# Layer norms of a decoder step: centring on TensorE, next weights split before the last tile, affine on ScalarE, mean shift inside the chain

## The chip, the cores and the metric

The kernel runs on one core of a Trainium2 chip as a single launch. A core has TensorE (PE, matrix products), VectorE (DVE), ScalarE (ACT), GpSimd (POOL) and SyncE (SP, which here issues most DMAs). The metric is device time in microseconds for one execution; the median of three runs is given for the kernel before.

## The reference

One inference step of a two-layer decoder, for 256 prompt tokens and 8 sample tokens together (264 columns). Model width 1024, FFN width 2816, four heads, 256 memory tokens.

```python
DN_ALPHA = (2 * DEPTH) ** 0.25                       # DEPTH = 2
def layer_norm(x, g, b):
    mu = jnp.mean(xf, -1, keepdims=True)
    var = jnp.mean(jnp.square(xf - mu), -1, keepdims=True)
    return (xf - mu) * lax.rsqrt(var + LN_EPS) * g + b
def trunk(x, ...):
    for l in range(DEPTH):
        x = layer_norm(DN_ALPHA * x + 0.5 * swiglu(x, gate[l, 0], up[l, 0], down[l, 0]), ln_g[l, 0], ln_b[l, 0])
        if l % 2 == 0: mix = gdn_conformer_mixer(x, ...)      # gated DeltaNet beside a convolution module
        else:          mix, gm_v = chunk_mlp_mixer(x, ...)    # gMLP with spatial gating
        x = layer_norm(DN_ALPHA * x + mix, ln_g[l, 1], ln_b[l, 1])
        x = layer_norm(DN_ALPHA * x + cross_attend(x, ...), ln_g[l, 2], ln_b[l, 2])
        x = layer_norm(DN_ALPHA * x + 0.5 * swiglu(x, gate[l, 1], up[l, 1], down[l, 1]), ln_g[l, 3], ln_b[l, 3])
```

Outputs are the new x of both groups, the keys and values of the memory, and the new states of the mixer. So there are eight layer norms over x. The text numbers them 0 to 7: norms 0, 3, 4 and 7 stand behind an FFN, norms 1, 2, 5 and 6 behind an output projection (mixer, attention 0, gMLP, attention 1).

## The kernel before

x lies transposed: eight tiles k = 0..7 of 128 channels by 264 tokens. Every large product is done in float32 accuracy by three products of rounded parts. A weight column block `raw` (1024 x 256, loaded by SP, three buffers) is cut into units of 128 output channels; ScalarE rounds one to `whi` (L221), VectorE or GpSimd subtracts and gives `wlo` (L222), with four buffers of each. The right-hand side is `xhi`, `xlo` likewise. A unit is 24 products on TensorE (8 tiles k, three each, L605) into one of four PSUM buffers `mm`, so a unit can start only when the unit four before it has been read out of PSUM.

A norm (class `Norm`) goes like this.

- `add` (L282) puts alpha times x plus the PSUM of output tile k into x. At k = 1 a rough mean is taken from the first two tiles (one product with `ones`, L289); ScalarE copies it twice, as `lnca` and `lnc` (L292, L293), GpSimd subtracts `lnca` from the six tiles still to come (L295), VectorE `lnc` from the first two (L297). `acc` then makes `xpre` (x times the gain, hi on ScalarE L313 and lo on VectorE L314) and adds to the running sums `lnS` (L320) and `lnQ` (squares, L319 and L321; the last two tiles on VectorE, the earlier ones on GpSimd).
- `finish` lets the next layer's products start on `xpre` before the norm is known: the true result is linear in it, so that a unit's PSUM is mended afterwards (`fixed`: L345 adds the mean's part, L346 multiplies by 1/sigma). Units 0 to 3 and some fillers (key and value products of a cross-attention, "K units", `Filler`) run there. After 18 products of unit 0 come the `sums`: three transposes of `lnS` (L149), the product that gives the remaining mean shift `dl` (L330), three transposes of `lnQ`. VectorE, with one square root on ScalarE (L110), turns them into 1/sigma as a diagonal `dg` (L135), and one product L137 spreads it over all partitions; it is called the spread below.
- Behind the spread x is made whole: x plus `lndl` (L367; VectorE for k < 2, GpSimd for the other six), times 1/sigma (L383), `xhi` with gain and bias (ScalarE L384), x itself with gain and bias (ScalarE L386; for k = 0, 2, 5 VectorE L392), `xlo` (L394; GpSimd for k = 3, 5, 7). Between them stand the fixes of units 0 to 7 at the steps `at`, and units 4 to 7 open as the fixes free their PSUM.
- `split_w` takes entries of the list `after_norm`: the `wlo` of two of units 0 to 3 goes to GpSimd (of 2 and 3, in front of an FFN of 1 and 3); the first two weights split after a norm wait until the square root and `dg` have been issued.

Each engine works its instructions off in order. That order is the program's, except where a scheduler at build time moves instructions; `pin` keeps those named in program order. The last norm has its own end (`finish_out`) and no `xpre`.

## Time and profile before

| | |
|---|---|
| median of 3 runs | 1422.63 us (1422.1 to 1422.78) |
| profiled execution, its own time | 1418.37 us |
| its span in the trace | 1416.6 us |
| granted TensorE clock, mean over the span | 0.975 of full |
| busy: PE, DVE, ACT, POOL | 1345.7, 952.9, 735.6, 317.1 us |

The profile is one execution; all durations below are from it, and it took 4.26 us less than the median. PE stands for TensorE's products, a window gives for each engine its busy time and in brackets the number of instructions that were recorded, then the granted TensorE clock, where 1.00 is the level of 2.4 GHz and 0.50 that of 1.2 GHz. "[1.89 <-DVE dg L135]" behind an instruction says that its engine had been idle for 1.89 us and what ended this.

### The profile page before, as it was taken

The numbers are of one execution on the slowest core, as the hardware profiler recorded it, in microseconds if no ns is written. First come the engines' busy times: TensorE is split into PE (matmuls) and PEld (weight loads), VectorE is DVE, ScalarE is ACT, GpSimd is POOL, SyncE is SP. The second block draws the span as 40 slices with busy tenths as digits, with TensorE's granted clock in tenths as the row PEclk, the third lists the DMA queues.
The fourth block names the chain that finished last, engine by engine and source line by source line (L and its number), as shares of the span: only waits on it lengthen the run. The fifth ranks groups of instructions, "written<-read, shape, count | busy, mean of one in ns | idle before, by whom it ended". The sixth has DMA issues, their size and how long they took to land.

```text
span 1416.6 us, 27334 instructions
## 1 busy us (share of the span) xinstructions
PE 1345.7 (95%) x10931; PEld 1276.2 (90%) x10931; DVE 952.9 (67%) x1845; ACT 735.6 (52%) x1343; POOL 317.1 (22%) x346
## 2 busy tenths in 40 slices
PE   8999998999998999799999999998898899899997
PEld 8999998876788979799999999998898868899996
DVE  5555667973867777965566765566789877955454
ACT  4545455785465535654444654444675625644432
POOL 3313313301231203411122211122414104311021
PEclk9999999899899999999999999999999999999998
DMA  7655664545668886355554565556539692565551
GB/s 257 211 179 173 222 192 135 160 135 162 201 211 284 289 288 210 119 183 185 191 175 160 173 218 185 182 174 187 158 127 302 222 321 77 175 213 179 176 170 44
DMA packets 270543, 269.27 MB, mean 190 GB/s; under 512 B 8243, under 2 KB 266291, under 8 KB 270400
## 3 DMA queue, kind: packets, MB, share of 16 engines
q1 hardware_dynamic: 257408, 260.97, 58.2%
q10 hardware_dynamic: 13008, 6.55, 1.7%
q8 instruction: 86, 1.41, 0.4%
q14 instruction: 41, 0.34, 0.1%
HBM read 252.81 MB, written 15.26 MB: 189 GB/s over the span
## 4 chain that ended last, share of the span: by engine, by line
PE 79%; DVE 13%; ACT 3%; issue 2%; DMA 2%; POOL 0%; SPq 0%; POOLq 0%; DVEq 0%; ACTq 0%
PE mm L605 47%; PE mm L230 6%; PE mm L229 6%; PE mm L231 6%; PE mm L656 3%; DVE wlo L222 3%; PE ax L1623 1%; ACT whi L221 1%; DVE xpre L314 1%; PE ax L1577 1%; DMA S_s<-in_state_dn_S_dram 1%; PE ax L1598 1%; PE mm L877 1%; PE ax L1556 1%; DVE lnS L320 1%
## 5 line engine op out<-in xcount | busy, mean ns | idle before, releaser
L222 DVE TENSOR_TENSOR wlo<-raw,whi 128x1024 fp32r<-128x1024 f32 (+1 forms) x374 | 455.2, 1221 | 269.9 <-ACT whi L221 269.1
L221 ACT CAST whi<-raw 128x1024 fp32r<-128x1024 f32 (+1 forms) x388 | 398.8, 1033 | 416.7 <-PE mm L605 211.6
L605 PE MATMUL mm<-xhi,whi 128*128 128x264 f32 x1728 | 493.6, 287 | 3.0 <-ACT whi L221 2.6
L605 PE MATMUL mm<-xhi,wlo 128*128 128x264 f32 x1728 | 493.4, 286 | 1.8 <-DVE wlo L222 1.8
L605 PE MATMUL mm<-xlo,whi 128*128 128x264 f32 x1728 | 493.8, 286 | 1.1 <-DVE xlo L184 1.0
L605 PEld LDWEIGHTS mm<-xhi,whi 128*128 128x128 f32 x1728 | 326.6, 190 | 6.8 <-ACT whi L221 3.2
L605 PEld LDWEIGHTS mm<-xhi,wlo 128*128 128x128 f32 x1728 | 326.0, 189 | 6.0 <-DVE wlo L222 3.4
L605 PEld LDWEIGHTS mm<-xlo,whi 128*128 128x128 f32 x1728 | 327.6, 190 | 3.6 <-DVE xlo L184 1.6
L229 PE MATMUL mm<-hh,whi 128*128 128x264 f32 x704 | 200.9, 285 | 0.0
L230 PE MATMUL mm<-hl,whi 128*128 128x264 f32 x704 | 199.6, 284 | 0.0
L231 PE MATMUL mm<-hh,wlo 128*128 128x264 f32 x704 | 199.5, 283 | 0.0
L605 PE MATMUL mm<-xpre,whi 128*128 128x266 f32 x768 | 148.8, 293 | 7.3 <-DVE xpre L314 3.0
L184 POOL TENSOR_TENSOR hl<-sg,hh 128x264 fp32r<-128x264 f32 x44 | 63.1, 1434 | 358.9 <-ACT hh L177 348.8
L230 PEld LDWEIGHTS mm<-hl,whi 128*128 128x128 f32 x704 | 132.6, 188 | 0.1
L229 PEld LDWEIGHTS mm<-hh,whi 128*128 128x128 f32 x704 | 132.5, 188 | 0.1
L231 PEld LDWEIGHTS mm<-hh,wlo 128*128 128x128 f32 x704 | 132.1, 188 | 0.0
L605 PEld LDWEIGHTS mm<-xpre,whi 128*128 128x128 f32 x768 | 122.7, 193 | 9.4 <-DVE xpre L314 3.9
L605 PE MATMUL mm<-xpre,wlo 128*128 128x266 f32 x384 | 110.8, 289 | 0.0
L295 POOL TENSOR_TENSOR x<-x,lnca 128x264 f32<-128x264 f32 x48 | 44.0, 951 | 239.4 <-ACT lnca L292 239.4
L605 PEld LDWEIGHTS mm<-xpre,wlo 128*128 128x128 f32 x384 | 73.7, 192 | 0.1
L321 POOL TENSOR_TENSOR lnQ<-lnQ,lnsq 128x264 f32<-128x264 f32 x40 | 42.6, 1064 | 105.8 <-ACT lnsq L319 105.4
L709 DVE TENSOR_TENSOR sg<-mm,sg 128x264 f32<-128x264 f32 x76 | 32.8, 432 | 47.3 <-PE mm L605 46.6
(479 smaller groups left out, 1870.7 us busy)
## 6 DMA issues: line engine op xcount, KB each, us to landing
raw<-in_ffn_w_gate_dram SPq DMA_DIRECT2D x43, 1024.0 KB, 6.6
raw<-in_ffn_w_up_dram SPq DMA_DIRECT2D x43, 1024.0 KB, 5.4
raw<-in_ffn_w_down_dram SPq DMA_DIRECT2D x32, 1024.0 KB, 5.2
cache<-in_cache_mem_k_dram SPq DMA_DIRECT2D x32, 512.0 KB, 6.4
cache<-in_cache_mem_v_dram SPq DMA_DIRECT2D x32, 512.0 KB, 4.2
raw<-in_ffn_w_down_dram SPq DMA_DIRECT2D x16, 768.0 KB, 4.6
raw<-in_ab_w_in_dram SPq DMA_DIRECT2D x12, 1024.0 KB
raw<-in_xa_wk_dram SPq DMA_DIRECT2D x8, 1024.0 KB, 5.3
```

The lines of the kernel that those rows point to most:

```text
L184: e.tensor_tensor(out=lo, in0=src, in1=f32(hi), op=ALU.subtract)
L221: A.copy(hi[:, :nk], r)
L222: e.tensor_tensor(out=lo[:, :nk], in0=r, in1=f32(hi[:, :nk]), op=ALU.subtract)
L229: PE.matmul(ps, lhsT=hi[:, k, :], rhs=xh, start=first, stop=False)
L230: PE.matmul(ps, lhsT=hi[:, k, :], rhs=xl, start=False, stop=False)
L231: PE.matmul(ps, lhsT=lo[:, k, :], rhs=xh, start=False, stop=last)
L295: G.tensor_tensor(out=x[:, j, :], in0=x[:, j, :], in1=ca, op=ALU.subtract)
L314: V.scalar_tensor_tensor(out=lo, in0=x[:, k, :], scalar=g, in1=f32(hi), op0=ALU.mult, op1=ALU.subtract)
L321: (V if k >= KT - 2 else G).tensor_tensor(out=Q, in0=Q, in1=sq, op=ALU.add)
L605: pin(PE.matmul(self.ps, lhsT=self.w[q // 2][:, k, :], rhs=self.rhs[q % 2][:, k, :], start=self.n == 1, stop=self.n == 3 * KT), pinned)
L656: pin(PE.matmul(self.ps[:, a * 256:(a + 1) * 256], lhsT=(mhi, mhi, mlo)[q][:, k, a * P:(a + 1) * P], rhs=self.w[k // 4][q % 2][:, k % 4, : ...
L709: V.tensor_tensor(out=sg, in0=pu, in1=sg, op=ALU.mult)
```

## The change

1. *Centring on TensorE* for norms 1, 2, 5 and 6 (`on_pe`). The rough mean is kept as a rounded pair `lncc` (64 partitions), and one more product with the constant `mrow` puts its negative into the PSUM of tiles k = 3 to 7, just before the last product of that tile's unit. The GpSimd subtractions L295 go there; tile 2 is centred by VectorE. All norms subtract straight from PSUM for tiles 0 and 1, and the copy `lnc` goes.
2. *Next weights earlier.* `early` splits the weights of the next units 0 and 1 before the last output tile; additions, sums and squares of the last two tiles are pinned in an order that puts `lnS` and `lnQ` ahead of `xpre` lo. The low parts of units 2, 3 and of the fillers are put off (`late`) behind `dg`, on VectorE; these units take their 16 products with `whi` first and the 8 with `wlo` after. No `wlo` goes to GpSimd any more.
3. *Affine on ScalarE, `xlo` and `lndl` on VectorE.* All eight L386 are ScalarE's, all `xlo` VectorE's. `lndl` is copied ahead of the square root, three of the subtractions stand inside the chain to `dg`, and the other five behind it, all on VectorE.
4. Sums: the transposes of `lnQ` come before the product `dl`. 18 products are pinned before the sums and 22 or so between them and the spread. A dummy activation loads the next function's table right behind the square root.

Three places in the instruction order follow. On VectorE, the end of the output projection in front of norm 2 (x is the tile sum, `mm_7060` and `mm_7071` the PSUM of the last output tile, `lnS`, `lnQ` the running sums, `tsum` the first step behind them). Before:

```order
L314 SCALAR_TENSOR_TENSOR xpre_6778<-x_114,par_110,xpre_6777 128x264
L282 SCALAR_TENSOR_TENSOR x_114<-x_114,mm_7024 128x264
L320 TENSOR_TENSOR lnS_6775<-lnS_6775,x_114 128x264
L222 TENSOR_TENSOR wlo_7120<-raw_7107,whi_7119 128x1024
L314 SCALAR_TENSOR_TENSOR xpre_6778<-x_114,par_110,xpre_6777 128x264
L321 TENSOR_TENSOR lnQ_6776<-lnQ_6776,lnsq_7052 128x264
L282 SCALAR_TENSOR_TENSOR x_114<-x_114,mm_7060 128x264
L320 TENSOR_TENSOR lnS_6775<-lnS_6775,x_114 128x264
L314 SCALAR_TENSOR_TENSOR xpre_6778<-x_114,par_110,xpre_6777 128x264
L321 TENSOR_TENSOR lnQ_6776<-lnQ_6776,lnsq_7088 128x264
L151 TENSOR_REDUCE tsum_7150<-ax_7146 128x3
L151 TENSOR_REDUCE tsum_7158<-ax_7154 128x3
```

And after:

```order
L311 SCALAR_TENSOR_TENSOR x_116<-x_116,mm_7022 128x264
L358 TENSOR_TENSOR lnS_6776<-lnS_6776,x_116 128x264
L360 TENSOR_TENSOR lnQ_6777<-lnQ_6777,lnsq_7049 128x264
L352 SCALAR_TENSOR_TENSOR xpre_6779<-x_116,par_112,xpre_6778 128x264
L311 SCALAR_TENSOR_TENSOR x_116<-x_116,mm_7071 128x264
L358 TENSOR_TENSOR lnS_6776<-lnS_6776,x_116 128x264
L360 TENSOR_TENSOR lnQ_6777<-lnQ_6777,lnsq_7098 128x264
L352 SCALAR_TENSOR_TENSOR xpre_6779<-x_116,par_112,xpre_6778 128x264
L154 TENSOR_REDUCE tsum_7148<-ax_7144 128x3
L154 TENSOR_REDUCE tsum_7154<-ax_7150 128x3
```

The split of the third unit's weights (`wlo_7120`) is gone from between the last two tiles, and `lnQ` stands ahead of `xpre` lo for both; GpSimd splits nothing beside it.

On TensorE, the last output tile of the same projection (`mm_7060`, in the change `mm_7071`) and the start of the next unit 0. Before:

```order
L605 MATMUL mm_7060<-xhi_5860,whi_7056 128x264
L605 MATMUL mm_7060<-xlo_5861,whi_7056 128x264
L605 MATMUL mm_7060<-xhi_5860,wlo_7057 128x264
L605 MATMUL mm_7127<-xpre_6777,whi_7109 128x266
L605 MATMUL mm_7127<-xpre_6778,whi_7109 128x266
L605 MATMUL mm_7127<-xpre_6777,wlo_7110 128x266
```

And after:

```order
L650 MATMUL mm_7071<-xhi_5861,whi_7055 128x264
L650 MATMUL mm_7071<-xlo_5862,whi_7055 128x264
L304 MATMUL mm_7071<-lncc_6848,mrow_90 128x264
L650 MATMUL mm_7071<-xhi_5861,wlo_7056 128x264
L650 MATMUL mm_7125<-xpre_6778,whi_7061 128x266
L650 MATMUL mm_7125<-xpre_6779,whi_7061 128x266
L650 MATMUL mm_7125<-xpre_6778,wlo_7062 128x266
```

One product with `lncc` and `mrow` stands before the tile's last one; there are five in each of four projections. The next unit's products follow as before.

On VectorE, what stands behind the diagonal `dg` of norm 2 (`raw` and `wlo` by number; `fix_7274` and `fix_7276` mend unit 0, `ax_7179` and `ax_7202` are the spread's result). Before:

```order
L135 TENSOR_SCALAR dg_7175<-ident_75,ra_y_7166 128x128 x2
L135 TENSOR_SCALAR dg_7175<-ident_75,ra_y_7166 128x8
L222 TENSOR_TENSOR wlo_7282<-raw_7279,whi_7281 128x1024
L346 TENSOR_TENSOR fix_7274<-fix_7274,ax_7179 128x264
L383 TENSOR_TENSOR x_114<-x_114,ax_7179 128x264 x3
L222 TENSOR_TENSOR wlo_7330<-raw_7327,whi_7329 128x1024
L392 TENSOR_SCALAR x_114<-x_114,par_110 128x264
L394 TENSOR_TENSOR xlo_7271<-x_114,xhi_7270 128x264
L345 SCALAR_TENSOR_TENSOR fix_7321<-lndl_7181,fixw_7319,mm_7195 128x264
L346 TENSOR_TENSOR fix_7321<-fix_7321,ax_7179 128x264
L383 TENSOR_TENSOR x_114<-x_114,ax_7179 128x264
L711 SCALAR_TENSOR_TENSOR sg_7277<-fix_7321,fixw_7319,sg_7277 128x264
```

And after:

```order
L138 TENSOR_SCALAR dg_7198<-ident_75,ra_y_7166 128x128 x2
L138 TENSOR_SCALAR dg_7198<-ident_75,ra_y_7166 128x8
L215 TENSOR_TENSOR wlo_7120<-raw_7059,whi_7119 128x1024
L215 TENSOR_TENSOR wlo_7123<-raw_7065,whi_7122 128x1024
L417 TENSOR_TENSOR x_116<-x_116,lndl_7158 128x264 x5
L386 SCALAR_TENSOR_TENSOR fix_7276<-lndl_7158,fixw_7274,mm_7125 128x264
L215 TENSOR_TENSOR wlo_7284<-raw_7281,whi_7283 128x1024
L387 TENSOR_TENSOR fix_7276<-fix_7276,ax_7202 128x264
L432 TENSOR_TENSOR x_116<-x_116,ax_7202 128x264 x3
L437 TENSOR_TENSOR xlo_7273<-x_116,xhi_7272 128x264
L386 SCALAR_TENSOR_TENSOR fix_7324<-lndl_7158,fixw_7322,mm_7181 128x264
L387 TENSOR_TENSOR fix_7324<-fix_7324,ax_7202 128x264
```

Two put-off `wlo` and five subtractions of `lndl` now stand between `dg` and the first fix; the affine L392 is gone from the row.

The core of the diff:

```diff
+    mrow = const.tile([64, P], F32R, name="mrow")
+    V.tensor_scalar(out=mrow, in0=ones[1][:64], scalar1=-1.0 / 32, scalar2=None, op0=ALU.mult)
...
-    def split_w(rw, j, rows=False):
+    def split_w(rw, j, rows=False, late=None):
...
-                n, ia, iv = after_norm.pop(0)
-                if n < 0:
-                    pass
-                elif n < 2:
-                    e = G
-                else:
-                    late.enter_context(tc.issue_after(ia))
-                    late.enter_context(tc.issue_after(iv))
+                for i in after_norm.pop(0):
+                    wait.enter_context(tc.issue_after(i))
             A.copy(hi[:, :nk], r)
-            e.tensor_tensor(out=lo[:, :nk], in0=r, in1=f32(hi[:, :nk]), op=ALU.subtract)
+            if late is None:
+                low()
+            else:
+                late.append(low)
...
+        def early(self):
+
+            if self.pre:
+                self.units = [self.unit(n) for n in range(2)]
+
+        def centre(self, k):
+
+            if k < 3 or not self.on_pe:
+                return None
+            return lambda ps: PE.matmul(ps, lhsT=mrow, rhs=self.cc, start=False, stop=False)
...
-                c1 = work.tile([P, T], F32, tag="lnc1", name="lnc1", bufs=1)
-                ca = work.tile([P, T], F32, tag="lnca", name="lnca", bufs=1)
-                A.mul(ca, cp[:, :T], 1.0 / self.a)
-                A.copy(c1, cp[:, :T])
-                for j in range(2, KT):
-                    G.tensor_tensor(out=x[:, j, :], in0=x[:, j, :], in1=ca, op=ALU.subtract)
-                for j in range(2):
-                    V.tensor_tensor(out=x[:, j, :], in0=x[:, j, :], in1=c1, op=ALU.subtract)
+                if self.on_pe:
+
+                    self.cc = work.tile([64, T], F32R, tag="lncc", name="lncc", bufs=1)
+                    A.copy(self.cc, cp[:64])
+                    V.tensor_tensor(out=self.cc[32:64], in0=cp[32:64], in1=f32(self.cc[32:64]), op=ALU.subtract)
...
+            for j in (0, 1) if k == 1 else (2,) if k == 2 and self.on_pe else ():
+                V.tensor_tensor(out=x[:, j, :], in0=x[:, j, :], in1=self.cp, op=ALU.subtract)
...
+            pin(V.tensor_tensor(out=S, in0=x[:, 0, :] if k == 1 else S, in1=x[:, k, :], op=ALU.add), last)
+            e = V if last else G
+            pin(e.tensor_tensor(out=Q, in0=Q, in1=sq, op=ALU.add), last)
+            if last:
+                low()
...
-            filler.products(18)
+            filler.products(18, True)
             self.sums(True)
-            y = self.rstd()
-            filler.products(2)
-            self.r = spread(y[:, 0:1], y[:, 1:2], y[:, 2:3], True)
             self.ndl = work.tile([P, T], F32, tag="lnca", name="lndl", bufs=1)
             A.mul(self.ndl, self.dl, -1.0)
+            y = self.rstd()
...
+            filler.products(22, True)
+            self.r = spread(y[:, 0:1], y[:, 1:2], y[:, 2:3], True)
             for k in range(KT):
-                (V if k < 2 else G).tensor_tensor(out=x[:, k, :], in0=x[:, k, :], in1=self.ndl, op=ALU.add)
-            filler.products(0, True)
+                with ExitStack() as wait:
+                    if k >= 3:
+                        wait.enter_context(tc.issue_after(chain["V"]))
+                    if k == 3:
+                        for low in late:
+                            low()
+                    V.tensor_tensor(out=x[:, k, :], in0=x[:, k, :], in1=self.ndl, op=ALU.add)
...
-                    if k not in (0, 2, 5):
-                        A.activation(out=xk, in_=xk, func=AF.Identity, scale=g, bias=b)
+                    A.activation(out=xk, in_=xk, func=AF.Identity, scale=g, bias=b)
...
-                    if j in (0, 2, 5):
-                        pin(V.tensor_scalar(out=xk, in0=xk, scalar1=g, scalar2=b, op0=ALU.mult, op1=ALU.add), True)
-                    e = G if j in (3, 5, 7) else V
-                    pin(e.tensor_tensor(out=rhs[1][:, j, :], in0=xk, in1=f32(rhs[0][:, j, :]), op=ALU.subtract), e is V)
+                    pin(V.tensor_tensor(out=rhs[1][:, j, :], in0=x[:, j, :], in1=f32(rhs[0][:, j, :]), op=ALU.subtract), True)
...
-            self.rows = range(KT)
+
+            self.order = [(k, q) for k in range(KT) for q in range(2 if hi_first else 3)] + [(k, 2) for k in range(KT) if hi_first]
...
-        nrm = Norm(idx, ALPHA, LN_EPS)
-        proj(src, 0, KT, rhs, nrm.add, rows)
+        nrm = Norm(idx, ALPHA, LN_EPS, units, True)
+        proj(src, 0, KT, rhs, nrm.add, nrm, rows)
```

## Rows read from the trace of the kernel before

**Rows 1.** The page: busy time by engine (section 1), chain by engine (section 4).

```profile
PE 1345.7 (95%) x10931; PEld 1276.2 (90%) x10931; DVE 952.9 (67%) x1845; ACT 735.6 (52%) x1343; POOL 317.1 (22%) x346
...
PE 79%; DVE 13%; ACT 3%; issue 2%; DMA 2%; POOL 0%; SPq 0%; POOLq 0%; DVEq 0%; ACTq 0%
```

**Rows 2.** TensorE's waits: who waits, for whom, total us, times, longest.

```profile
PE ax L137 <- DVE dg L135: 21.0, 7, 4.9
```

**Rows 3.** Windows, tails of four output projections: length, busy us (count), clock.

```profile
431.00:441.00 10.00, 6.70 (x26) 5.55 (x26) 8.92 (x17) 4.51 (x10) 1.81 (x2) 0.66 0.98 310
568.00:578.00 10.00, 4.78 (x26) 4.25 (x25) 8.81 (x15) 3.21 (x8) 4.96 (x5) 0.83 0.64 207
1087.00:1093.00 6.00, 3.51 (x15) 2.56 (x15) 5.44 (x10) 2.76 (x7) 0.97 (x2) 0.72 1.08 349
1193.00:1208.00 15.00, 10.68 (x60) 9.83 (x60) 14.62 (x20) 8.29 (x17) 9.26 (x5) 0.77 0.41 128
```

**Rows 4.** Windows around four spreads, the last at full clock.

```profile
219.00:229.00 10.00, 5.47 (x25) 5.06 (x24) 6.67 (x12) 2.81 (x6) 4.46 (x5) 0.68 0.06 12
989.00:1001.00 12.00, 7.09 (x36) 6.71 (x35) 8.25 (x16) 5.12 (x9) 5.25 (x5) 0.72 0.28 89
1096.00:1104.00 8.00, 4.21 (x21) 3.93 (x21) 6.06 (x13) 1.62 (x3) 4.41 (x4) 0.79 0.60 191
778.00:785.00 7.00, 4.46 (x36) 4.24 (x35) 5.32 (x11) 4.95 (x6) 1.96 (x3) 1.00 0.00 0
```

**Rows 5.** Timeline before norm 2: start us, length us, engine, line, idle before.

```profile
570.66 2.43 POOL L222 TENSOR_TENSOR wlo<-raw,whi 128x1024 fp32r<-128x1024 f32 x1 [1.60 <-ACT whi L221]
...
570.81 2.56 DVE L321 TENSOR_TENSOR lnQ<-lnQ,lnsq 128x264 f32<-128x264 f32 x1
...
574.24 0.90 PE L149 MATMUL ax<-ident,lnS 128*128 128x128 f32 x3 [5.22 <-DVE lnS L320]
```

**Rows 6.** TensorE timeline at norm 6: first sum, next product, spread.

```profile
1206.97 0.49 PE L149 MATMUL ax<-ident,lnS 128*128 128x128 f32 x3
...
1207.99 0.49 PE L605 MATMUL mm<-xpre,whi 128*128 128x266 f32 x2
...
1213.96 0.71 PE L137 MATMUL ax<-dg,ones 128*128 128x264 f32 x2 [2.52 <-DVE dg L135]
```

**Rows 7.** Window behind the spread of norm 2.

```profile
584.00:600.00 16.00, 16.00 (x132) 16.00 (x131) 13.78 (x30) 14.19 (x29) 4.73 (x3) 1.00 0.42 133
```

**Rows 8.** Timeline behind the spread of norm 2, TensorE and VectorE.

```profile
582.21 0.68 PE L137 MATMUL ax<-dg,ones 128*128 128x264 f32 x2 [1.89 <-DVE dg L135]
...
589.47 0.49 DVE L711 SCALAR_TENSOR_TENSOR sg<-fix,fixw,sg 128x264 f32<-128x264 f32 x1
...
589.88 0.43 DVE L394 TENSOR_TENSOR xlo<-x,xhi 128x264 fp32r<-128x264 f32 x1
...
590.22 0.42 DVE L383 TENSOR_TENSOR x<-x,ax 128x264 f32<-128x264 f32 x1
...
590.88 1.22 DVE L222 TENSOR_TENSOR wlo<-raw,whi 128x1024 fp32r<-128x1024 f32 x1
...
592.02 0.43 DVE L394 TENSOR_TENSOR xlo<-x,xhi 128x264 fp32r<-128x264 f32 x1
...
599.47 0.48 DVE L345 SCALAR_TENSOR_TENSOR fix<-lndl,fixw,mm 128x264 f32<-128x264 f32 x1
...
601.05 0.29 PE L605 MATMUL mm<-xhi,whi 128*128 128x264 f32 x1
```

**Rows 9.** Groups by line: shapes, count, busy us, mean ns.

```profile
L367 POOL TENSOR_TENSOR x<-x,lndl 128x264 f32<-128x264 f32 x42 | 34.7, 857 | 31.6 <-ACT lndl L365 31.6
...
L392 DVE TENSOR_SCALAR x<-x,par 128x264 f32<-128x264 f32 x21 | 9.2, 438 | 2.0 <-ACT xhi L384 2.0
...
L386 ACT ACTIVATE x<-x,par 128x264 f32<-128x264 f32 x35 | 20.8, 605 | 0.2
...
L221 ACT CAST whi<-raw 128x1024 fp32r<-128x1024 f32 x356 | 372.3, 1051 | 375.6 <-PE mm L605 211.6 <-PE mm L230 82.6 <-issue 50.4
```

More of the change, by code (lines that the diff above doesn't have):

```diff
@@ L237, in proj, with proj_units, make, unit @@
             for j in range(2):
+                n = n2 * 2 + j
                 u = Unit(split_w(rw, j), rhs)
[L239 to L256 removed]
+                u.order = [(k, q) for k in rows for q in range(3)]
+                if nrm is not None and n == KT - 1:
+                    nrm.early()
+                u.products(3 * KT, centre=nrm and nrm.centre(n))
+                evac(n, u.ps)
+    def proj_units(src, c0, act=None):
+        def make(pre):
+            rw = {}
+            def unit(n, late=None):
+                if n % 2 == 0:
+                    rw[n // 2] = load_w(src, KT, c0[n // 2])
+                return Unit(split_w(rw[n // 2], n % 2, late=late), pre, late is not None)
+            return unit
+        return make, act
+    def ffn_units(l, i):
+        def make(pre):
+            rw = {}
+            def unit(u, late=None):
+                n = u // 2
+                if n % 2 == 0:
+                    rw[u] = load_w((ffn_w_gate, ffn_w_up)[u % 2][l, i], KT, n * P)
+                return Unit(split_w(rw[u - n % 2 * 2], n % 2, late=late), pre, late is not None)
+            return unit
+        return make, AF.Silu
     class Norm:
[L267 removed]
+        def __init__(self, idx, scale, eps, units=None, on_pe=False):
+            pre = units is not None
+            units, self.act = units or (None, None)
+            self.on_pe = on_pe
             self.idx, self.a, self.eps = idx, scale, eps
@@ L281, in add @@
         def add(self, k, ps):
-            V.scalar_tensor_tensor(out=x[:, k, :], in0=x[:, k, :], scalar=self.a, in1=ps, op0=ALU.mult, op1=ALU.add)
+            last = k >= KT - 2
+            pin(V.scalar_tensor_tensor(out=x[:, k, :], in0=x[:, k, :], scalar=self.a, in1=ps, op0=ALU.mult, op1=ALU.add), last)
             if k == 0:
@@ L309, in acc @@
                     PE.transpose(self.xt[c, k // 4][:, k % 4 * P:(k % 4 + 1) * P], x[:, k, TOK[c]], ident)
+            sq = Q if k == 0 else work.tile([P, T], F32, tag="lnsq", name="lnsq")
+            if last:
+                pin(A.activation(out=sq, in_=x[:, k, :], func=AF.Square))
             if self.pre:
@@ L600, in products @@
                     self.open()
-                k, q = divmod(self.n, 3)
-                k = self.rows[k]
+                k, q = self.order[self.n]
                 self.n += 1
+                if centre and self.n == 3 * KT:
+                    centre(self.ps)
                 m -= 1
@@ L748, in ffn @@
                 up(n2 * 2 + j, sg, uu.ps)
-        nrm = Norm(idx, 2 * ALPHA, 4 * LN_EPS, not last)
+        last = units is None
+        nrm = Norm(idx, 2 * ALPHA, 4 * LN_EPS, units)
         if last:
```

148 lines of the change are left out of this document (70 added, 78 removed).

## The prediction

> **What bounds the kernel now.** I read the page first: TensorE is busy for 95% of the span and carries 79% of the chain that ended last, VectorE 13% [rows 1]. So time is won only where TensorE stands idle or runs at the lower clock, and lost wherever another engine comes to hold it up. Next came TensorE's waits: the longest entry by far is the spread L137 waiting for `dg`, 21.0 us at seven norms [rows 2]. The rest that the change can reach lies in front of the sums, so I took windows around the tails of the four output projections (norms 1, 2, 5, 6). Length less busy time gives the idle time: 10.00 - 6.70 = 3.30, 5.22, 2.49 and 4.32 us, in all 15.3 us [rows 3]. The same rows show the clock: it averages 0.66 to 0.83, so parts of these tails run at 1.2 GHz. What that costs I take from the count. At full clock 132 products take 16.00 us, 0.1212 us each [rows 7]. In the first window 26 took 6.70 us where 3.15 would do, 3.55 us too much; the others give 1.63, 1.69 and 3.41, in all 10.3 us [rows 3]. A few records can be missing from a trace, so I count 9.7. The same sum for the spreads of norms 0, 4 and 5 gives 2.44, 2.73 and 1.66, together 6.8 us; norm 3's spread had a gap too, and the clock stayed at 1.00 [rows 4].
>
> **Part by part, against the profiled execution (1418.37 us).**
>
> *The sums.* Before norm 2 GpSimd's `wlo` took 2.43 us from 570.66, and VectorE's `lnQ` beside it 2.56 us [rows 5], against about 0.34 us for such an operation in a dense row (590.22 less 589.88, [rows 8]). TensorE then idled 5.22 us for the sums [rows 5]. The change takes both sources away: no `wlo` on GpSimd, and `lnS` and `lnQ` ahead of `xpre` lo. Behind the last product of the last tile VectorE needs the addition, `lnS`, and, with ScalarE's square between them, `lnQ`. With one more `whi` (1051 ns, [rows 9]) in ScalarE's queue ahead of that square this is about 1.9 us; the 18 pinned products and the three transposes of `lnS` cover 18 x 0.1212 + 0.3 = 2.5 us. So the 15.3 us of idle time go, and the 9.7 us with them: **-25.0 us**.
>
> *The spread.* In the undisturbed case, norm 6, 6.99 us pass from the first transpose (1206.97) to the spread (1213.96), with the sums taking 1.02 us of TensorE [rows 6]. The chain of the change has as many steps: a subtraction of `lndl` stands where a fix stood. I take 6.9. TensorE now has 23 products there, 2.8 us, so 6.9 - 1.0 - 2.8 = 3.1 us are open at each norm, 7 x 3.1 = 21.7 us against 21.0 [rows 2]: +0.7. Norms 0 and 4, where GpSimd's split stretched `dg`, gain; norms 1 and 2 lose. A gap of 3.1 lies between norm 3's (7.00 - 4.46 = 2.54, clock kept) and norm 5's (8.00 - 4.21 = 3.79, clock lost) [rows 4]. I let half of seven lose it, 3.5 x 2.3 (the mean of the three) = 8.0 against 6.8. Together **+1.9**; from all kept (-6) to all lost (+10).
>
> *The centring products.* 20 more on TensorE, of a kind that the trace does not show (64 rows of weights in place of 128). Not below 0, not above twice an ordinary product. I take the ordinary price, 20 x 0.1212 = **+2.4** (0 to 4.8). The subtractions that they replace were GpSimd's beside other work; TensorE did not wait for them there.
>
> *Behind the spread.* Here the change costs. GpSimd's six subtractions (857 ns each, [rows 9]) and three `xlo` become VectorE's, and two to five put-off `wlo` come right behind `dg`; against this only three L392 leave. Take norm 2. In dense rows `wlo` costs 1.14 us, a two-input operation with a scalar 0.41, one without 0.34 (differences of starts in [rows 8]). Before, from `dg` to the fix that frees the PSUM of unit 4, VectorE has 5 `wlo`, 6 of the second and 21 of the third kind: 5.7 + 2.5 + 7.1 = 15.3 us. It took 17.7 (582.21 to 599.95), 2.4 of it waits, mostly for ScalarE, while TensorE, fed from the spread at 582.21 on, needed that buffer only at 601.05, 18.8 us on [rows 8]. After, the same stretch has 8 `wlo`, 7 and 26: 9.1 + 2.9 + 8.8 = 20.8 us. TensorE's stock is as before, 18.8 us. With no waits the fix is 2.0 us late, with those of before 4.4; since a longer queue takes up a little of the waiting I take 4.0. ScalarE itself was busy for 14.19 of 16.00 us there [rows 7] and gets three affines (605 ns, [rows 9]) less a table load that moves into the chain's gap: as near its limit as VectorE, which is why I keep waits in. Norm 6 leads into the same kind of FFN and costs the same, 4.0. Attention 1 (norm 5) has less stock, but VectorE idled there for 1.94 of 8.00 us [rows 4]; by the same count its last `xlo` comes 23 us behind `dg`, 25 with waits, and I estimate 3 us late (0 to 6). The gMLP (norm 4) and the mixer (norm 0) get 1 each: around `dg` VectorE idled 3.75 of 12.00 and 3.33 of 10.00 us [rows 4], which takes much of the work up. Attention 0 and FFN 2 (norms 1, 3) have some 250 products in stock, 30 us: nothing. Sum **+13** (6 to 25). These stalls can drop the clock; one falls, **+2.5** (0 to 11).
>
> *Held at nothing.* The `lncc` pieces, tile 2's subtraction and the dropped `lnc` copies stand in the middle of output projections, where VectorE has room. `early` moves the splits of units 0 and 1, not their loads: SP's queue issues the weight loads in the order of before but for a few swaps. At some norms a filler's `whi` now stands before the square root on ScalarE and waits for unit 0's buffer, free 1.0 + 6 x 0.1212 = 1.7 us into the chain of 6.9; I take its 1.05 us as hidden in the steps up to the root, and if its load were late, the chain would be longer by that.
>
> Sum: -25.0 + 1.9 + 2.4 + 13 + 2.5 = -5.2, so 1413.2 for an execution like the profiled one. This lies 4.26 us under the median of the runs, so **1417.4 us**.
>
> **A rule that speaks on this.** Beside GpSimd's split of 2.43 us VectorE's small operation took 2.56 [rows 5]. The Trainium skill, page "SBUF — State Buffer", section "SBUF: two separate sides", says why: the two engines share a pair of ports that is locked for a whole instruction, and the other fully blocks. The page "Perfetto Trace Analysis", section "Optimizing Scalar/DVE Operations", adds that offloading between the two "might not help" for that reason. Read the other way round, work taken from GpSimd to VectorE would cost VectorE little, since it was blocked for it already. That is the first rival. Row against it: in the stretch behind the spread VectorE's L392 took 438 ns on average [rows 9], close to its undisturbed length, so there was little blocking to win back.
>
> **Rivals.**
>
> *Nothing is lost behind the spread.* VectorE gets rid of waits for GpSimd's `xlo` and `lndl` and of blocked stretches (GpSimd was busy for 4.73 us of the 16.00 in [rows 7]), and holds the fixes in time. Then the 13 and the 2.5 fall away: 1413.2 - 15.5 = 1397.7, or 1402 as a median. For it: TensorE kept going there before with VectorE busy 13.78 of 16.00. Against it: the counts above, 20.8 us of work for 18.8 us.
>
> *The clock comes back as a loss at the spreads.* All seven gaps of 3.1 us end with TensorE at 1.2 GHz, at 2 us each: 14.0 in place of 8.0, and -5.2 becomes +0.8: 1423.4, no change that can be measured. For it: norm 5's gap in front of the sums was only 2.49 us and its window averaged 0.72 [rows 3]. Against it: norm 3.
>
> *VectorE becomes the bound behind every spread.* Several `wlo` stand ahead of a tile's product with 1/sigma; each waits for a `whi` on ScalarE, which waits for TensorE to free a buffer, which waits for a fix that is queued behind that `wlo` on VectorE. Where this ring closes, the lags add up instead of overlapping: 2 us more at each of the five norms and three more falls of the clock, +10 and +7 on top of 15.5, so that +11.8 comes out: 1430 for the profiled run, 1434 as a median. It decides from the point where stalls behind the spread and their clock exceed 20.7 us, what the rest gains. For it: ScalarE 14.19 and VectorE 13.78 of 16.00 before any work was added. Against it: the fixes of units 5 to 7 follow at less than a unit's 2.9 us.
>
> **How the numbers follow.** Forecast 0.42, with a range of its own of 1411 to 1421 (0.40 of it faster, 0.02 no change); nothing lost behind the spread 0.15 (faster); clock lost at the spreads 0.20 (same); VectorE as the bound 0.23 (slower). 0.2% or 2.8 us is about what a measurement here tells from no change. Faster 0.55, same 0.22, slower 0.23. The range of 1404 to 1431 us leaves out about half of the first rival and a good third of the last.
>
> **What would show it.** Right: TensorE's wait for `lnS` gone, the windows in front of norms 1, 2, 5 and 6 at clock 1.00; seven spread gaps of about 3 us each, all alike; a new wait of TensorE's first product with `xhi` behind norms 2 and 6, for the fix of VectorE; GpSimd's busy time well under 250 us. Wrong: gaps still in front of the sums (the 18 products do not cover), spread gaps of 4 us and more (ScalarE's order in the chain), or no new wait behind norms 2 and 6.

## The result, and the profile after

The changed kernel took a median of 1409.93 us (four runs, 1408.96 to 1411.27) against 1422.37 us for the kernel before beside it (1417.62 to 1422.78): a ratio of 0.9921 with an interval of 0.9897 to 0.9944. So it is faster by 0.8%, 12.4 us. Between the two profiled executions, 1418.37 and 1408.96 us, the gain is 9.4 us where the sum said 5.2. Sign and range held; the terms behind them did not all, and large errors of opposite sign hide in the total.

The page after, busy time by engine and the chain by engine, answers to [rows 1]:

```profile
PE 1346.6 (96%) x10951; PEld 1274.7 (91%) x10951; DVE 940.6 (67%) x1910; ACT 742.0 (53%) x1362; POOL 200.8 (14%) x245
...
PE 63%; DVE 9%; ACT 6%; DMA 4%; issue 2%; POOL 0%; SPq 0%; POOLq 0%; ACTq 0%; DVEq 0%
```

TensorE's busy time hardly moved; its idle time (span less busy) went from 70.9 to 60.6 us. TensorE's waits after (who waits, for whom, total us, times, longest) answer to [rows 2]:

```profile
PE mm L650 <- DVE fix L386: 11.4, 6, 3.4
...
PE mm L650 <- ACT whi L222: 5.2, 4, 1.7
PE ax L1450 <- DMA wsn<-in_gm_w_s_dram: 4.9, 1, 4.9
```

Of the 21.0 us for `dg` 0.9 are left. New at the top is `fix`, for which no product waited before, and `wsn`, the gMLP's spatial weights, has grown from 1.8 us.

Windows around the tails of the same four output projections as in [rows 3] (length; busy us with counts of PE, PEld, DVE, ACT, POOL; clock; DMA share; GB/s):

```profile
424.00:436.00 12.00, 12.00 (x91) 11.19 (x91) 10.09 (x19) 8.17 (x14) 2.42 (x3) 1.00 0.83 269
556.00:569.00 13.00, 13.00 (x99) 12.17 (x99) 10.44 (x19) 8.52 (x14) 2.92 (x3) 1.00 0.27 83
1079.00:1090.00 11.00, 11.00 (x82) 10.12 (x81) 7.76 (x15) 6.11 (x12) 1.53 (x2) 1.00 1.01 325
1183.00:1195.00 12.00, 11.36 (x83) 10.11 (x82) 11.89 (x21) 8.16 (x15) 3.93 (x5) 1.00 0.28 88
```

TensorE is busy throughout in three of them and idle for 0.64 us in the last; the clock is 1.00 in all four. This part did what the prediction said.

The two timelines at norm 6, which the prediction took as its undisturbed case [rows 6], first before (start us, length us, engine, line, idle time before it):

```profile
1208.41 4.82 POOL L367 TENSOR_TENSOR x<-x,lndl 128x264 f32<-128x264 f32 x6 [2.27 <-ACT lndl L365]
1209.45 0.71 DVE L337 SCALAR_TENSOR_TENSOR lnm<-tsum,lnm 128x3 f32<-128x3 f32 x1
...
1211.88 0.67 DVE L113 TENSOR_TENSOR ra_t<-ra_t,ra_y 128x3 f32<-128x3 f32 x1
```

and after:

```profile
1193.82 0.52 PE L152 MATMUL ax<-ident,lnS 128*128 128x128 f32 x3 [0.64 <-DVE lnS L358]
...
1196.27 0.15 DVE L378 SCALAR_TENSOR_TENSOR lnm<-tsum,lnm 128x3 f32<-128x3 f32 x1
...
1197.35 0.16 DVE L116 TENSOR_TENSOR ra_t<-ra_t,ra_y 128x3 f32<-128x3 f32 x1
...
1197.74 0.62 DVE L138 TENSOR_SCALAR dg<-ident,ra_y 128x128 f32<-128x128 f32 x3
1198.42 0.71 PE L140 MATMUL ax<-dg,ones 128*128 128x264 f32 x2
```

The same steps on 128x3 numbers took 0.67 and 0.71 us while GpSimd subtracted `lndl`, and take 0.15 to 0.16 us without it. From the first transpose (1193.82) to the spread (1198.42) 4.60 us pass in place of 6.99; the 23 products and the sums' own work on TensorE fill that, so no gap is left (the spread's row shows no idle time). At norms 0, 4 and 5, where the clock had fallen behind the gap, it is 1.00 in the 8 to 10 us from the spread on (windows 217 to 227, 994 to 1002 and 1090 to 1098).

Where the span went is seen best when it is cut at the spreads of norms 0 to 6. The stages, first before (columns as above):

```profile
223.90:446.10 222.20, 205.49 (x1863) 177.17 (x1863) 158.53 (x429) 138.73 (x314) 48.75 (x66) 0.93 0.59 177
...
780.70:994.80 214.10, 207.38 (x1702) 206.53 (x1703) 135.19 (x181) 106.44 (x165) 41.19 (x34) 1.00 0.59 185
...
1214.00:1416.60 202.60, 192.97 (x1571) 190.34 (x1571) 116.46 (x163) 92.10 (x143) 32.85 (x29) 0.98 0.50 157
```

and after:

```profile
217.00:439.60 222.60, 202.67 (x1858) 173.65 (x1858) 157.90 (x439) 140.21 (x319) 31.52 (x50) 0.94 0.59 176
...
772.70:993.80 221.10, 211.62 (x1701) 210.20 (x1701) 133.01 (x190) 107.83 (x169) 27.06 (x22) 0.98 0.57 179
...
1198.40:1407.20 208.80, 195.79 (x1582) 193.05 (x1581) 121.35 (x171) 94.07 (x148) 28.75 (x26) 0.97 0.51 162
```

All eight stages in order, after less before, in us: -6.9 (FFN 0, up to norm 0's spread), +0.4 (mixer), -2.9 (attention 0), +1.4 (FFN 1), +7.0 (FFN 2), -5.8 (gMLP), -8.8 (attention 1), +6.2 (FFN 3). Stages that end in an output projection's norm gain, except the mixer's; FFNs that stand behind a spread lose. FFN 2's loss is not of one kind: the longer wait for `wsn` lies in it too, and without that wait the stage took 212.0 us, less than before (the edit on `wsn` below).

What an FFN loses by its fixes is seen behind the spread of norm 2 (timeline, which answers to [rows 8]):

```profile
593.62 1.23 DVE L215 TENSOR_TENSOR wlo<-raw,whi 128x1024 fp32r<-128x1024 f32 x1
594.76 0.43 DVE L437 TENSOR_TENSOR xlo<-x,xhi 128x264 fp32r<-128x264 f32 x1
595.11 0.48 DVE L386 SCALAR_TENSOR_TENSOR fix<-lndl,fixw,mm 128x264 f32<-128x264 f32 x1
595.74 0.36 PE L650 MATMUL mm<-xhi,whi 128*128 128x264 f32 x1 [2.73 <-DVE fix L386]
```

VectorE works through `wlo` and `xlo` without a pause, and the fix that frees a PSUM buffer stands behind them: TensorE waits 2.73 us. Such waits came at norm 0 (0.96 and 0.34), 2 (2.73), 3 (2.71), 4 (1.23) and 6 (3.40), none at norm 5. Behind the three long ones the clock fell (windows):

```profile
594.00:602.00 8.00, 6.26 (x39) 6.30 (x40) 6.66 (x12) 4.03 (x8) 0.38 (x1) 0.79 0.61 188
807.00:815.00 8.00, 6.04 (x38) 6.07 (x39) 6.67 (x12) 4.15 (x8) 0.16 (x1) 0.79 0.65 202
1220.00:1228.00 8.00, 5.94 (x38) 5.97 (x39) 6.62 (x11) 4.24 (x7) 0.10 (x1) 0.79 0.92 305
```

By 0.1212 us a product they cost 1.53, 1.43 and 1.34, together 4.3 us.

### The profile page after: what moved, and what is told of

Its sections match the earlier page's. It is cut to its first block, busy times and chain, and to the rows that moved or that the text cites. A ratio compares the mean times of both kernels' runs of the same rounds, so it can differ in the third digit from the quotient of the medians.

```text
span 1407.2 us, 27349 instructions
## 1 busy us (share of the span) xinstructions
PE 1346.6 (96%) x10951; PEld 1274.7 (91%) x10951; DVE 940.6 (67%) x1910; ACT 742.0 (53%) x1362; POOL 200.8 (14%) x245
## 4 chain that ended last, share of the span: by engine, by line
PE 63%; DVE 9%; ACT 6%; DMA 4%; issue 2%; POOL 0%; SPq 0%; POOLq 0%; ACTq 0%; DVEq 0%
PE mm L650 37%; PE mm L808 4%; PE mm L807 4%; PE mm L809 4%; PE mm L702 3%; DVE wlo L215 3%; ACT whi L222 2%; PE ax L1669 1%; PE ax L1623 1%; DMA S_s<-in_state_dn_S_dram 1%; PE ax L1644 1%; PE ax L1602 1%; DMA atts<-kT 1%; ACT xhi L433 1%; DVE xlo L437 1%
## 5 line engine op out<-in xcount | busy, mean ns | idle before, releaser
L215 DVE TENSOR_TENSOR wlo<-raw,whi 128x1024 fp32r<-128x1024 f32 (+1 forms) x388 | 470.5, 1221 | 262.0 <-ACT whi L222 259.9
L650 PEld LDWEIGHTS mm<-xhi,whi 128*128 128x128 f32 x1728 | 328.2, 190 | 19.2 <-ACT whi L222 15.7
L650 PE MATMUL mm<-xpre,whi 128*128 128x266 f32 x768 | 136.6, 292 | 2.5 <-DVE fix L386 2.5
L650 PEld LDWEIGHTS mm<-xpre,whi 128*128 128x128 f32 x768 | 115.7, 191 | 3.9 <-ACT whi L222 1.4
L650 PE MATMUL mm<-xpre,wlo 128*128 128x266 f32 x384 | 95.6, 290 | 1.8 <-DVE wlo L215 1.8
L650 PEld LDWEIGHTS mm<-xpre,wlo 128*128 128x128 f32 x384 | 67.1, 191 | 2.8 <-DVE wlo L215 2.5
L1607 DVE CUSTOM_DVE_ANT_0 junk<-cache,ax 128x256 f32<-128x256 f32 x128 | 46.1, 414 | 6.0 <-PE ax L1602 5.9
```

What stands on the lines that cost most here:

```text
L215: e.tensor_tensor(out=lo[:, :nk], in0=r, in1=f32(hi[:, :nk]), op=ALU.subtract)
L650: pin(PE.matmul(self.ps, lhsT=self.w[q // 2][:, k, :], rhs=self.rhs[q % 2][:, k, :], start=self.n == 1, stop=self.n == 3 * KT), pinned)
L1607: V.tensor_tensor_reduce(out=junk, in0=kc[:, b, a, :], in1=pq[:, b * 256:(b + 1) * 256], scale=1.0, scalar=0.0, op0=ALU.mult, op1=ALU.add, ...
```

## Experiments

Every ratio is to the kernel before on the same chip, with its 95% interval.

### GpSimd keeps the subtraction of lndl (changed kernel)

The `dg` gaps had gone though 3.1 us were expected at each norm. Theory: GpSimd's two-input subtractions had slowed VectorE's small steps in the chain, before. Rival: the new order of the chain made it shorter. Here the new order stays, and six of the eight subtractions go back to GpSimd, which starts them when `lndl` is there, as before the change. The put-off `wlo` then follow `dg` directly.

```
-                    if k >= 3:
-                        wait.enter_context(tc.issue_after(chain["V"]))
                     if k == 3:
-                        for low in late:
-                            low()
-                    V.tensor_tensor(out=x[:, k, :], in0=x[:, k, :], in1=self.ndl, op=ALU.add)
+                        with tc.issue_after(chain["V"]):
+                            for low in late:
+                                low()
+                    (V if k < 2 else G).tensor_tensor(out=x[:, k, :], in0=x[:, k, :], in1=self.ndl, op=ALU.add)
```

> The kernel after, with six of the eight subtractions of the mean shift (lndl) given back to GpSimd, as before the change; the put-off low parts stay behind dg. Theory (contention): the small steps of the chain from the sums to dg on VectorE (128x3 elements, about 0.16 us each in the kernel after, about 0.66 in the one before) were stretched by GpSimd's subtractions running beside them. Then they take 0.4 to 0.7 us again, the chain from the first transpose to the spread grows from 4.6 to about 7 us, TensorE's wait for dg grows from 0.9 to about 20 us over seven norms, and the median rises by 10 to 25 us, less what VectorE saves behind the spreads. Rival (order): the chain is short because the fix left it, lndl is copied earlier and the sums of lnQ come first; then the small steps stay near 0.16 us, the wait for dg stays under 4 us, and the median falls by a few us, since VectorE has 42 operations less.

1432.67 us, 1.0094 (1.0074 to 1.0113): slower than the kernel before. TensorE's waits:

```profile
PE ax L140 <- DVE dg L138: 20.7, 8, 3.1
PE mm L649 <- DVE fix L386: 5.7, 4, 2.7
```

The seven gaps at the spreads were 2.78 to 3.06 us each, and in the chain at norm 6 the slow steps are back:

```profile
1217.61 2.70 POOL L416 TENSOR_TENSOR x<-x,lndl 128x264 f32<-128x264 f32 x3 [6.25 <-ACT lndl L401]
1218.65 0.71 DVE L378 SCALAR_TENSOR_TENSOR lnm<-tsum,lnm 128x3 f32<-128x3 f32 x1
...
1221.06 0.67 DVE L116 TENSOR_TENSOR ra_t<-ra_t,ra_y 128x3 f32<-128x3 f32 x1
...
1223.14 0.71 PE L140 MATMUL ax<-dg,ones 128*128 128x264 f32 x2 [3.06 <-DVE dg L138]
```

The theory holds. The gap of 3.1 us a norm in the prediction is what the change gives if GpSimd keeps `lndl`; the new order alone closes none of these gaps.

### The subtraction of lndl on VectorE alone (kernel before)

The same edit in the other direction, with nothing else of the change. The six subtractions change their engine and wait for `dg`.

```
 for k in range(KT):
-    (V if k < 2 else G).tensor_tensor(out=x[:, k, :], ...)
+    with ExitStack() as wait:
+        if k >= 2:
+            wait.enter_context(tc.issue_after(chain["V"]))
+        V.tensor_tensor(out=x[:, k, :], ...)
```

> The kernel before, with one edit: the six subtractions of lndl that GpSimd had go to VectorE, behind dg. Theory (contention): the small steps of the chain shrink to about 0.16 us except where GpSimd's weight split runs beside them, TensorE's wait for dg falls from 21 us to 3 to 8 us, and new waits for fixes behind the spreads appear; the median falls by 5 to 15 us. Rival (order): the wait for dg stays above 15 us, and the median is the same or higher.

1400.98 us against 1419.75, 0.9864 (0.9841 to 0.9886). TensorE's wait for `dg` fell from 21.0 to 1.3 us, that for `lnS` stayed, and for a fix one product waited, 0.4 us. The expected 5 to 15 us were too few, and the expected waits for fixes did not come. First the waits, then VectorE's steps in the chain at norm 6:

```profile
PE ax L149 <- DVE lnS L320: 7.6, 2, 5.2
```

```profile
1194.04 0.16 DVE L113 TENSOR_TENSOR ra_t<-ra_t,ra_y 128x3 f32<-128x3 f32 x1
```

This one edit takes 18.8 us off, more than the whole change, whose remaining parts, on top of it, therefore cost some 8 us net (0.9921 less 0.9864, of 1420).

### GpSimd's wlo on VectorE alone, and both edits (kernel before)

The other disturbance that the prediction named is GpSimd's split beside the sums [rows 5].

```
 elif n < 2:
-    e = G
+    e = V
```

> The kernel before, with one edit: the 14 weight splits that GpSimd had go to VectorE, in their old places; lndl stays on GpSimd. Theory: the waits in front of the sums (15 us) fall below 6, the three spreads beside a split (norms 0, 4 and 5: 4.5, 4.9 and 3.8 us) fall to the 2.5 us of norms 3 and 6, and the median falls by 10 to 17 us. Rival: 14 x 1.14 us more on VectorE in the tails keep the sums as late as GpSimd's blocking did; waits in front of the sums stay above 10 us and the median falls by less than 4.

1405.93 us, 0.9903 (0.9884 to 0.9922). The `dg` wait fell to 11.8 us and `lnS` to 4.8; a fix wait of 2.0 appeared. In front of the sums some 10.5 of the 15.3 us of idle time stood in their old places, where under 6 had been expected: 3.3 at norm 1, 2.40 at norm 2 (from 5.22), 2.38 at norm 5 and 2.5 at norm 6 (from 4.3). With the edit on `lndl` as well:

> The kernel before, with two edits and nothing of the rest of the change: lndl on VectorE behind dg (as in the run before), and the 14 weight splits that GpSimd had on VectorE as well. Theory (contention explains the sums too): the waits in front of the sums at norms 1, 2, 5 and 6 fall from 15 us to under 6, the waits for dg stay under 3 us, no wait for a fix above 2 us appears, and the median lies 6 to 15 us below that of the edit of lndl alone, near 1390. Rival: VectorE's additional splits arrive late instead and the tails keep 10 us of waits; then the median is that of lndl alone or up to 5 us higher.

1394.3 us, 0.9814 (0.9793 to 0.9834), half a per cent under the edit on `lndl` alone. What was left in front of the sums again did not vanish as expected (TensorE's waits):

```profile
PE ax L149 <- DVE lnS L320: 4.8, 2, 2.4
```

So GpSimd's splits account for about a third of the idle time in front of the sums: at norm 1 three gaps (1.70, 0.60 and 1.07 us, before 1.45, 0.60 and 1.07) stand with its splits and its `lndl` both gone. That part of the expectation was wrong. The changed kernel has none of these gaps, but how much of that is its order is not shown: GpSimd still centres the tiles here, and VectorE's `xpre` lo (L314) still took 0.98 us at the median of 56, against 0.48 at the least.

### No centring product (changed kernel)

```
-    nrm = Norm(idx, ALPHA, LN_EPS, units, True)
+    nrm = Norm(idx, ALPHA, LN_EPS, units)
```

> The kernel after, with the centring on TensorE undone alone: norms 1, 2, 5 and 6 subtract the rough mean with GpSimd again as the FFN norms do; the 20 extra products are gone. By the prediction's own step (20 x 0.12 us, the subtractions held at nothing) the median falls by about 2.4 us. Rival: GpSimd's 24 subtractions stretch VectorE's operations beside them in the output projections (about 0.9 us where 0.42 is usual), VectorE falls behind, and waits of TensorE for lnS or xpre come back in front of the sums: 3 to 10 us slower.

1410.3 us, 0.9933 (0.9917 to 0.9950), not told apart from 0.9921 (0.9897 to 0.9944), so neither the expected gain nor the rival's loss came. The row of the 20 products in the changed kernel (one line's instructions: min/median/max ns), and the last of them in TensorE's timeline:

```profile
L304 PE MATMUL mm<-lncc,mrow x20: 383/383/387, 418.7 to 1190.2; 64*128 64x264 f32 x20
```

```profile
1190.02 0.28 PE L650 MATMUL mm<-xlo,whi 128*128 128x264 f32 x1
1190.23 0.38 PE L304 MATMUL mm<-lncc,mrow 64*128 64x264 f32 x1
1190.55 0.39 PE L650 MATMUL mm<-xhi,wlo 128*128 128x264 f32 x1
1190.77 0.41 PE L650 MATMUL mm<-xpre,whi 128*128 128x266 f32 x2
```

From the product ahead of it to the one two places behind it 0.75 us pass, where two ordinary steps would take 0.24: it holds TensorE up by 0.51 us. The others show nearly the same starts, which makes some 10 us in all. Without them TensorE is busy 1341.8 us in place of 1346.6, only 4.8 less; but its clock was lower at the same time (0.978 of full over the span, against 0.981), which makes products longer. Its idle time is 5.2 us longer, since the subtractions are VectorE's or GpSimd's again:

```profile
PE mm L650 <- DVE wlo L215: 6.2, 6, 3.8
...
PE ax L152 <- DVE lnS L358: 3.0, 3, 1.9
```

So the products cost some 10 us of TensorE's time, and the waits and the clock that they save come to about as much.

### The gMLP's spatial weights transposed later (changed kernel)

In both kernels the load of `wsn` is issued at nearly the same moment, and the transposes that wait for it start 7.2 us later before and 6.5 us later after. Before (the issue, and the transposes):

```profile
978.03 0.53 SPq L1396 DMA_DIRECT2D wsn<-in_gm_w_s_dram  x1
...
985.25 0.63 PE L1404 MATMUL ax<-ident,wsn 128*128 128x128 f32 x4 [1.83 <-DMA wsn<-in_gm_w_s_dram]
```

After:

```profile
977.77 1.27 SPq L1442 DMA_DIRECT2D wsn<-in_gm_w_s_dram  x1
...
984.29 1.12 PE L1450 MATMUL ax<-ident,wsn 128*128 128x128 f32 x4 [4.88 <-DMA wsn<-in_gm_w_s_dram]
```

Before, 29 products of the next weights stood ahead of the transposes. The change pins 18 of these in front of the sums, so that they come behind the transposes, which are now the first thing behind the down projection. The clock fell behind the gap:

```profile
984.00:992.00 8.00, 7.71 (x43) 7.65 (x44) 2.73 (x10) 1.28 (x3) 0.00 (x0) 0.66 0.01 2
```

The edit moves the transposes behind the norm:

```
-        wsT = gp.tile([P, 4, P], F32, name="wsT")
-        pt = ax_ps()
-        for g in range(4):
-            PE.transpose(pt[:, g * P:(g + 1) * P], wsn[:, g, :], ident)
-        V.tensor_tensor(out=wsT, ...)
...
         rhs = nrm.finish(fillers, ev_v, (3, 4, 9, 9, 10, 12, 13, 13))
+        wsT = gp.tile([P, 4, P], F32, name="wsT")
+        ... (the same lines)
```

> The kernel after, with one edit: the four transposes of the gMLP's spatial weights (wsn) stand behind the norm's finish instead of in front of it. Theory: the pinning of the 18 products in front of the sums of norm 4 left these transposes as the first thing on TensorE behind the down projection, so that TensorE waits 4.9 us for a load that is issued at the same moment as before, and the clock falls behind it. Then the wait for wsn goes (4.9 us to 0), the clock stays at 1.00 there (some 2 us), and the median falls by 5 to 7 us against the kernel after. Rival: TensorE would have waited there anyway, for lnS or dg or for a weight that is just as late; then one wait takes the place of the other and the median moves by less than 2 us.

1401.67 us, 0.9871 (0.9857 to 0.9886): 0.50% of 1420, 7.1 us. The wait was gone, and the stage up to norm 4's spread took 212.0 us in place of 221.1.

### Fixes earlier; three xlo back on GpSimd; both with the wsn edit (changed kernel)

Theory: behind a spread VectorE has more work than TensorE's stock covers. Two ways to relieve it: put the fixes of an FFN's last units ahead of other work, or take work off. The rival for the second was that GpSimd would slow VectorE again.

```
-            src = src.finish(fillers, evac, (0, 3, 5, 5, 10, 11, 12, 13))
+            src = src.finish(fillers, evac, (0, 3, 5, 5, 8, 9, 10, 11))
```

> The kernel after, with one edit: in the FFN behind norms 2, 3 and 6 the fixes of units 4 to 7 stand at steps 8, 9, 10 and 11 in place of 10, 11, 12 and 13, so that the fix that frees the PSUM of unit 4 stands ahead of the last two xlo and of two weight splits on VectorE. Theory (queue position): that fix comes 2 x 0.34 + 2 x 1.14 = 3.0 us earlier, the three waits for it (2.7, 2.7 and 3.4 us) shrink to under 1 us each, and the median falls by 6 to 10 us, some of it from the clock. Rival (VectorE is short of time altogether): the waits turn into waits for xlo or wlo of the same total, and the median moves by less than 2 us.

1400.47 us, 0.9868 (0.9848 to 0.9889); the fix wait fell to 2.5 us, `wsn` rose to 6.5. Time and wait are as the theory expected.

```
-    pin(V.tensor_tensor(out=rhs[1][:, j, :], ...), True)
+    e = G if j in (3, 5, 7) else V
+    pin(e.tensor_tensor(out=rhs[1][:, j, :], ...), e is V)
```

> The kernel after, with one edit: xlo of tiles 3, 5 and 7 on GpSimd again. By the prediction's step behind the spreads (every operation counted at VectorE's dense price) VectorE has 3 x 0.34 = 1.0 us less per norm, the waits for fixes (11.4 us at six places) fall to about 6 to 8, and the median falls by 3 to 6 us. Rival (contention): GpSimd's xlo stretches VectorE's operations beside it, the waits for fixes stay at 10 us or more, and the median is the same or up to 6 us higher.

1399.48 us, 0.985 (0.9829 to 0.9872); fix wait 4.8 us; the gain on the changed kernel, 0.7%, is more than the 3 to 6 us expected. Neither the spread nor the fixes suffered. Behind the spread VectorE's operations are long and none has to end before the next link of a chain; that this is why GpSimd did no harm there is argued, not shown.

> The kernel after with two of the edits that helped alone: the transposes of wsn behind the norm, and the FFN fixes of units 4 to 7 two steps earlier. Theory (two separate losses): the gains add, about 7 us for each (0.9871 and 0.9868 against 0.9921 for the kernel after, as ratios to the one before), so a ratio near 0.982, with neither the wait for wsn nor a wait for a fix above 1.5 us. Rival (the second only moved TensorE's idle time to the wsn load, 4.9 to 6.5 us there): then the two together gain more than the sum, a ratio of 0.979 or less.

The wsn edit and the earlier fixes together: 1393.3 us, 0.9813 (0.9797 to 0.9830). The gains add, as expected (0.982).

> The kernel of the run before in this set, and xlo of tiles 3, 5 and 7 on GpSimd as well. If VectorE is still short of time behind the spreads, this gives another 2 to 4 us (ratio 0.978 to 0.980). Rival: with the fixes ahead of the last xlo nothing waits for VectorE any more and GpSimd's blocking of it shows; then the ratio is that of the run before or up to 0.002 higher.

With the three `xlo` on top: 1390.66 us, 0.9798 (0.9774 to 0.9822). The intervals overlap, so that last step is not shown.

### The splits not put off (changed kernel)

The put-off `wlo` stand right behind `dg`, ahead of the tiles' products and fixes.

```
-            fillers = kv_units(*kv, late)
-            units += [unit(n, late) for n in (2, 3)]
+            fillers = kv_units(*kv)
+            units += [unit(n) for n in (2, 3)]
```

> The kernel after, with one edit: the low parts of units 2 and 3 and of the fillers are not put off behind dg, and these units take their products in the usual order. Theory (the put-off splits, 2 to 5 x 1.14 us, are what makes the fixes late): the waits for fixes fall from 11.4 us to under 5; the splits go in front of or into the chain, whose length grows by up to 2 us, and the wait for dg comes back at some norms (3 to 10 us). Net within 5 us of the kernel after, either way. Rival (VectorE has the same work in either place): the waits for fixes stay at 9 us or more.

1397.15 us, 0.9837 (0.9819 to 0.9856), 0.84% under the changed kernel's ratio, 12 us, where at most 5 either way had been expected. TensorE's waits:

```profile
PE mm L650 <- DVE fix L386: 1.6, 3, 1.0
...
PE ax L152 <- DVE lnS L358: 3.0, 4, 1.7
```

The fix waits all but went and only 2.4 us of `lnS` came back; the `dg` wait did not. Only the first two stages grew by it (norm 0's spread came at 219.9 in place of 217.0, and the mixer's stage took 227.0 us in place of 222.6). So the last run puts splits off at norm 0 alone, with the wsn edit:

```
+            later = late if self.idx == 0 else None
+            fillers = kv_units(*kv, later)
+            units += [unit(n, later) for n in (2, 3)]
```

> The kernel after with two edits: the transposes of wsn behind the norm, and the put-off low parts kept at norm 0 alone (in front of the mixer, the stage that grew by some 7 us without them); everywhere else the splits stand where the run without put-off parts had them. Theory (both losses are separate and the put-off parts pay only at norm 0): stage by stage, the sum of the best stages is about 1382 us for the profiled run, a ratio of 0.974 to 0.978. Rival: the mixer grew for another reason than norm 0's put-off parts, or the waits move on; then the ratio stays at 0.980 or above.

1386.84 us, 0.9772 (0.9758 to 0.9786): faster than both kernels, by 2.3% and by some 21 us against the changed one. TensorE is busy for 97% of its span. The ratio is the expected one, but its reason is not shown: up to norm 1's spread 443.9 us pass, against 446.9 without any put-off splits and 439.6 in the changed kernel, so that less than half of that loss came back. The gain of the `wsn` edit (0.0050) would by itself bring the run without put-off splits from 0.9837 to 0.979, with an interval that reaches over 0.9772; so what norm 0's put-off splits give is not shown by the times.

## Why the prediction was right in size and wrong in its terms

**The sums, -25.0 us: right.** 15.3 us of idle time became 0.64, and the clock is 1.00 in all four tails. The prediction named two sources, GpSimd's split and VectorE's order. The split was the smaller part: with it gone some 10.5 of the 15.3 us stayed. A third source was held at nothing: with the centring back on GpSimd 6.8 us of waits stood in front of the sums and of a last tile's product (1.93, 0.51, 0.53 and 3.83), against 0.64.

**The spread, +1.9 us: wrong, and this is the step that failed.** "In the undisturbed case, norm 6, 6.99 us pass ... The chain of the change has as many steps" was read off a chain that was not undisturbed. GpSimd ran six subtractions beside it. Counting steps was right, pricing them from that row was not: with the 128x3 steps at 0.16 us the chain is 4.60 us long. The gaps fell from 21.0 to 0.9 us, and the clock no longer falls behind the spreads of norms 0, 4 and 5 (6.8 us before). Both directions were tried: GpSimd's `lndl` put back gives 2.78 to 3.06 us a norm, and taken out alone -18.8 us. The row to read was before the eyes: GpSimd's 4.82 us for six `lndl` lies across the steps. The prediction used the rule of the Trainium skill, page "SBUF — State Buffer", section "SBUF: two separate sides" (a GpSimd operation that reads SBUF and a VectorE operation with two inputs there, or one in a two-port mode, lock a shared pair of ports against each other for a whole instruction), for the sums and for the stretch behind the spread, and not for the chain, where it matters most. Here the trace agrees with it, at 0.5 us more for a step of 0.16 us, though VectorE's 128x264 subtraction, with two inputs in SBUF, kept its 0.42 us there.

**The centring products, +2.4 us: wrong on both sides.** They hold TensorE up by 0.51 us each, some 10 us, four times the price taken and twice the upper end given. That the old subtractions cost TensorE nothing was the other mistake: putting them back costs 5.2 us of waiting and a lower clock, and the two errors cancel in the time.

**Behind the spread, +13 and +2.5 us: right in sum, less so by place.** The fix waits came to 11.4 us and the three falls of the clock to 4.3, 15.7 in place of 15.5. Norm 6 took 3.40 of 4.0 and norm 2 2.73 of 4.0; norm 5's 3 did not come; norm 3, put at nothing for its stock of some 250 products, took 2.71. The stock was as counted; the window from the spread to that wait (columns as above) shows that it did not reach:

```profile
772.70:809.00 36.30, 31.94 (x254) 31.17 (x254) 26.85 (x48) 23.20 (x43) 1.22 (x1) 0.99 0.63 203
```

TensorE ran 254 products, and VectorE, busy for only 26.85 of 36.30 us, still came late: it had stood idle for 3.60 and 4.53 us earlier, waiting for ScalarE's `whi` (VectorE's timeline below), and had its work at the end. ScalarE in turn had waited for two weight loads, 1.91 and 1.43 us. Load was counted there, not order.

```profile
781.14 4.63 DVE L215 TENSOR_TENSOR wlo<-raw,whi 128x1024 fp32r<-128x1024 f32 x4 [3.60 <-ACT whi L222]
790.31 1.23 DVE L215 TENSOR_TENSOR wlo<-raw,whi 128x1024 fp32r<-128x1024 f32 x1 [4.53 <-ACT whi L222]
```

The first rival (nothing lost) fell with this. The cause is VectorE's load and order: the wait fell to 2.5 us with the fixes put earlier, 4.8 with three `xlo` elsewhere, 1.6 without put-off splits.

**Held at nothing: wrong for `wsn`.** The prediction considered the weight loads and SP's order, not what of TensorE's own work had stood between the load and its user. Taking the 29 products away from in front of the transposes cost 3.1 us of waiting and the clock, 7.1 us by the run.

**What stays open.** The mixer's stage should have lost the sums' 3.3 us and some clock, and grew by 0.4. TensorE's idle time in it went from 16.7 to 19.9 us. Since 3.3 in front of the sums and 0.9 at the spread are gone, 7.4 us came back; 1.3 of it are waits for fixes; the rest are new or longer waits, for `whi` (1.72 and 1.60 us), for `ba` (1.23) and for `S_s` among them. Its five centring products add 2.6 us of work. The order of its instructions is another, and the best kernel's mixer stage is no shorter (225.6 us). Which move causes these waits was not tried.

**The sum.** Split into idle and busy time of TensorE, the forecast was -1.6 (-15.3 + 0.7 + 13) and -3.6 us (-9.7 + 1.2 + 2.4 + 2.5); measured were -10.3 and +0.9. The spreads gave some 29 us more than forecast, idle time and clock together; `wsn`, the waits in the mixer and the centring products took most of that back. That the sum came within 4.2 us (-9.4 against -5.2) is luck: large errors of opposite sign met in it.

## What to carry to other kernels

Before a chain of tiny operations is priced from the trace, look at what the other engines do beside it: a case should be called undisturbed only if GpSimd's row is empty there, or if the steps are as short as elsewhere. A product of another shape is priced by the starts of its neighbours, not by the ordinary step. When work is pinned to cover one wait, list what it covered in its old place, loads included. A split that is put off behind a critical step lands in front of whatever waits next on that engine.
